# A decoder step with expert retrieval: 192 gathered tokens instead of 128, 352 columns through the whole tables instead of 416, three row buffers instead of two

## The chip, the cores and the metric

The kernel runs on one core of a Trainium2 chip. Its time is the device time of one execution in microseconds (us). The core has TensorE (PE, with its weight loads shown apart as PEld), VectorE (DVE), ScalarE (ACT), GpSimd (POOL), SyncE (SP, which issues most DMAs) and 16 DMA engines. Each engine works through its own list of instructions in order.

## The reference

One decoder layer for 544 tokens of width 2048: 512 tokens of a prompt and 8 x 4 sample tokens. First come a norm, an input projection, a gated MLP over positions, an RWKV-7 mixer and an output projection. Then comes the part that the change touches: `peer_ffn`, a product-key retrieval of experts, and after it a residual sum and a norm.

```python
q = (xt @ w_q).reshape(n_tok, 8, 2, 128)
s = einsum('nhcd,ckd->nhck', q, sub_keys)           # 2 x 128 key scores per head
top_s, top_i = top_k(s, 16)                         # then the best 16 of 16 x 16 sums
...
ue = u_tab[e_b]                                     # 16384 x 2048 table, 128 rows a token
act = gelu(einsum('nhkd,nd->nhk', ue, x_b))
coef = gates * act
out = einsum('nhk,nhkd->nd', coef, v_tab[e_b])
```

So each token needs 128 rows of `u_tab` (a dot product with its own normed activation) and the same 128 rows of `v_tab` (a weighted sum). Each table holds 134 MB in float32.

## The kernel before

The kernel has two ways to do this and splits the tokens between them.

**Whole tables (tokens 0 to 415, `T1` = 416 columns).** TensorE multiplies all 16384 rows with the 416 tokens, and a matrix of gates that is zero almost everywhere picks the few that count. The first table is read in 128 blocks of 128 experts (`activations`, L750): 48 matmuls of 416 columns a block, into one PSUM bank; DVE multiplies by the norm's factor (L755), ACT takes the gelu. The second table is read in 32 groups of 4 blocks and 8 pairs of column tiles (`products`, L1048): 24 matmuls of 416 columns a call, after which DVE adds two banks to `yT` (L1065). Between them `coefficients` (L1031) multiplies activations by gates on POOL (L1041) and splits them into two float32r parts (ACT L1044, POOL L1045). All weights go through `split` (L647): a DMA of 512 KB on SP's queue into one of three `wr` buffers, a cast on ACT (`wh`) and a subtraction on DVE (`wl`, L655). Each product is then three matmuls (hi x hi, hi x lo, lo x hi), which is why there are 48 and 24.

**Gathered rows (tokens 416 to 543, `TG` = 128).** They go in waves of 32 tokens (`gather_steps`, L776): 4 groups of slots x 32 tokens fill the 128 partitions, so that a wave has 32 steps on `u_tab` and 32 on `v_tab`. One step fetches 128 rows of 8 KB (1 MB) with an indirect DMA that POOL issues (`fetch`, L793), and works on the row block fetched the step before: `dot` (L805) or `add` (L813), one DVE instruction over 128 x 2048. There are two row buffers (`row`, bufs=2). Step 8 of the next wave runs `finish` (L838), which sums the four groups of slots with four small matmuls, adds the residual and norms; it takes two of the row buffers for its own operands, loaded through SP's queue.

**What sets the order.** `gathers(n, after)` (L866) counts fractions of steps and hands out a step when a whole number is reached; the fetch and the row's DVE instruction get a dependency on `after`, the DVE instruction that has just emptied a bank. A step is handed out for each early block (`EW` = 1); in the last stage the steps that are left are spread over `products` calls (weight 4) and `activations` calls (weight 6) with a factor `PACE` = 1.06, so that they end when 1/1.06 of the stage is done. A planner then orders each engine's list by priority.

**The stages behind the mixers.** 1159 to 1263 us: second half of the output projection, norm 2, the gathered tokens' rows written to memory (`hn` the residual, `xg` the normed row). 1263 to 1487: queries and scores; the last 128 tokens have theirs with tokens on partitions. 1487 to 1918: top-k of the other tiles on DVE; TensorE works on early blocks (`early`, L764; 52 blocks of the first table before their gates exist, written to `Cd`). 1918 to 2204: the gate matrix, in 13 groups of 32 tokens (L1002 to L1016: 16 comparisons on DVE, a multiplication on POOL, matmuls), each group followed by one early block. 2204 to 2254: the early blocks that are left. 2254 to the end: `coefficients` and `products`.

Of the kernel before, what the change touches and what calls it, by code (L numbers as in the profile page):

```python
# [15 lines left out]
D = 2048  # L16
# [12 lines left out]
# columns of the constants' array  # L29
# [38 lines left out]
def front(tc, I, O, SC, dbg=None):  # L68
    """norm1, input projection, both mixers; leaves y^T in SC['yT']."""
# [54 lines left out]
        # the sample's tokens; the states before them are normalised already  # L124
# [23 lines left out]
    def weights(src, k0, n):  # L148
        """part of a weight tile, split into two float32r parts that add up to it"""
# [9 lines left out]
    # ---------------- projection of one column tile: 2 halves in PSUM  # L159
# [16 lines left out]
    # ---------------- A: v half, LayerNorm, mixing over positions  # L176
# [88 lines left out]
    # halved biases for sigmoid(z) = 0.5 tanh(z/2) + 0.5  # L265
# [14 lines left out]
    def seg(p, s, q, lora, st):  # L280
# [17 lines left out]
        # decay: log w = -E05 sigmoid(.)  # L298
# [18 lines left out]
        # normalised kk  # L317
# [10 lines left out]
        # k (1 + (a - 1) k_a)  # L328
# [24 lines left out]
        # V with tokens on partitions: even head's rows 64.., odd head's rows ..64  # L353
# [19 lines left out]
        # B, K with tokens on partitions  # L373
# [7 lines left out]
        # inner products  # L381
        # E[:, 0] holds N^T on the rows of its head, E[:, 1] the keys' part on the other head's
# [37 lines left out]

        # L = ((I - N)^-1)^T by merging diagonal blocks, Ti = L^T
# [5 lines left out]
        # blocks of at most 32 rows: their transposes stay within the blocks  # L427
# [14 lines left out]
        # the states  # L442
# [63 lines left out]
        # group norm, bonus, gate  # L506
# [46 lines left out]
    # ---------------- h = x + y_A w_out[:W_A] + .., the first half of the sum  # L553
# [34 lines left out]
TG = 128  # L588
T1 = TC - TG
HT = TC // 2  # L590
NW = TG // 32
GT = 32
GB = 4
EARLY = 52
# [8 lines left out]
def back(tc, I, O, SC):  # L603
    """output projection, norm2, PEER, final norm."""
# [33 lines left out]
    # top-k results by token tile: gates and the two key numbers  # L638
# [8 lines left out]
    def split(wp, src, ahead, E=V):  # L647
        """1024 columns of weights, split into two float32r parts that add up to them"""
# [34 lines left out]
    ms = rsp.tile([TG, 1], F32, name="ms")  # L683
    with ExitStack() as s1:
# [5 lines left out]
        xh = x2.tile([128, KT, T1], F32R, name="xh2")  # L690
        xl = x2.tile([128, KT, T1], F32R, name="xl2")
        xt = pool(xts, "xt", side="right")
        th = xt.tile([128, KT, TG], F32R, name="th")
        tl = xt.tile([128, KT, TG], F32R, name="tl")
# [7 lines left out]
        hn = hp.tile([TG, D], F32, name="hn")  # L702
        ss = hp.tile([128, TC], F32, name="ss")
        for m in range(KT):
# [13 lines left out]
            if m % 4 == 0:  # L718
                pxt = px.tile([128, 512], F32, name="pxt")
# [5 lines left out]
            for hi, lo, c in ((xh, xl, slice(0, T1)), (th, tl, slice(T1, TC))):  # L725
# [7 lines left out]
        # the gathered tokens' rows, normalised  # L733
        G.dma_start(SC["hn"], hn)
# [474 lines left out]
```

## Time and profile before

| | us |
|---|---|
| time, median of 3 runs (lowest, highest) | 4234.88 (4228.41, 4239.51) |
| the profiled execution: span from first to last instruction | 4256.0 |
| PE busy | 3973.8 (93%) |
| PEld busy | 3741.6 (88%) |
| DVE busy | 2894.4 (68%) |
| POOL busy | 1508.2 (35%) |
| ACT busy | 1329.7 (31%) |
| mean granted TensorE clock | 0.969 |
| moved by DMA | 760.39 MB |

The profile's page gives one execution, and of that one only the span; no time outside the span is shown for it. Busy time of PE counts a matmul from its start to a modelled end, and matmuls overlap, so that a busy PE is not a PE at its peak: the number of matmuls in a stretch (the x behind its busy time) says more. The DMA share is the mean busy share of the core's 16 DMA engines.

### The profile page before, as it was taken

Reading aid. Unit: us, or ns where it says so; the run is one execution under the profiler, and the core shown is the slowest. Engines: PE = TensorE matmul, PEld = TensorE weight load, DVE = VectorE, ACT = ScalarE, POOL = GpSimd, SP = SyncE. Lnnn points to the kernel's source line nnn. Section 1 sums busy time; section 2 is a strip of 40 time slices with the busy share of each in tenths; the row PEclk is TensorE's granted clock in tenths of the full one; section 3 lists DMA queues with packets and bytes.
Section 4 is the critical chain, followed back from the end, with each engine's and each line's share of the span. In section 5 each row is a group of like instructions: output and inputs, shape, how many; then the busy total and the mean of one; then the engine's idle time right before and its main releaser. Section 6 shows DMA issues by size and latency. Waiting matters only on the chain. (4 is left out here: it accounts for less than half of the span.)

```text
span 4256.0 us, 65074 instructions
## 1 busy us (share of the span) xinstructions
PE 3973.8 (93%) x25618; PEld 3741.6 (88%) x25618; DVE 2894.4 (68%) x4763; ACT 1329.7 (31%) x2137; POOL 1508.2 (35%) x1222
## 2 busy tenths in 40 slices
PE   8999999999999988788889899999999999999997
PEld 8888888887999987787789899899898998999997
DVE  4566666666455599979984766666666666766754
ACT  4244444444232222223332222222222222322233
POOL 1212222222160056576653334343343333433323
PEclk9999999997999999999999999999999999999998
DMA  4311111112553245465566767777677776776752
GB/s 150 105 56 58 59 57 57 58 56 77 189 163 97 77 140 196 168 229 215 204 233 221 262 237 256 244 263 258 229 253 258 248 249 240 263 254 246 257 177 90
DMA packets 240241, 760.39 MB, mean 179 GB/s; under 512 B 23240, under 2 KB 88520, under 8 KB 204224
## 3 DMA queue, kind: packets, MB, share of 16 engines
q1 hardware_dynamic: 191136, 427.57, 30.9%
q0 software_dynamic: 48800, 328.67, 20.5%
q8 instruction: 202, 3.31, 0.3%
q14 instruction: 103, 0.84, 0.1%
HBM read 692.53 MB, written 63.61 MB: 178 GB/s over the span
## 5 line engine op out<-in xcount | busy, mean ns | idle before, releaser
L654 ACT CAST wh<-wr 128x1024 fp32r<-128x1024 f32 x560 | 581.5, 1048 | 1248.0 <-PE o L1057 545.7
L655 DVE TENSOR_TENSOR wl<-wr,wh 128x1024 fp32r<-128x1024 f32 x488 | 618.2, 1268 | 319.2 <-ACT wh L654 318.4
L668 PE MATMUL g<-xh,wh 128*128 128x416 f32 x2048 | 733.1, 358 | 67.1 <-DVE ac L755 67.0
L1057 PE MATMUL o<-ch,wh 128*128 128x416 f32 x2048 | 740.1, 361 | 48.3 <-ACT ch L1044 41.8
L1057 PE MATMUL o<-cl,wh 128*128 128x416 f32 x2048 | 740.1, 361 | 35.9 <-POOL cl L1045 35.9
L668 PE MATMUL g<-xh,wl 128*128 128x416 f32 x2048 | 733.9, 358 | 3.5 <-POOL wl L655 3.5
L1057 PE MATMUL o<-ch,wl 128*128 128x416 f32 x2048 | 733.5, 358 | 0.0
L668 PE MATMUL g<-xl,wh 128*128 128x416 f32 x2048 | 726.4, 355 | 0.0
L668 PEld LDWEIGHTS g<-xh,wh 128*128 128x128 f32 x2048 | 392.6, 192 | 78.1 <-issue 75.2
L1057 PEld LDWEIGHTS o<-ch,wh 128*128 128x128 f32 x2048 | 398.3, 194 | 64.3 <-ACT ch L1044 48.9
L1057 PEld LDWEIGHTS o<-cl,wh 128*128 128x128 f32 x2048 | 395.8, 193 | 47.5 <-POOL cl L1045 44.8
L805 DVE SCALAR_TENSOR_TENSOR row<-row,xrow 128x2048 f32<-128x2048 f32 x128 | 309.2, 2416 | 167.8 <-DMA row<-in_u_tab,idx 166.8
L1057 PEld LDWEIGHTS o<-ch,wl 128*128 128x128 f32 x2048 | 396.3, 194 | 7.3
L793 POOL DMA_INDIRECT row<-in_v_tab,idx x128 | 231.4, 1808 | 480.6 <-DVE y L1065 295.4
L668 PEld LDWEIGHTS g<-xh,wl 128*128 128x128 f32 x2048 | 391.5, 191 | 8.6 <-POOL wl L655 5.2
L668 PEld LDWEIGHTS g<-xl,wh 128*128 128x128 f32 x2048 | 392.8, 192 | 6.4
L813 DVE SCALAR_TENSOR_TENSOR acc<-row,dots,acc 128x2048 f32<-128x2048 f32 x124 | 296.3, 2389 | 147.4 <-DMA row<-in_v_tab,idx 145.5
L171 PE MATMUL g<-xh,wh 128*128 128x276 f32 x1248 | 379.3, 304 | 10.0 <-ACT xh L113 10.0
L793 POOL DMA_INDIRECT row<-in_u_tab,idx x128 | 221.8, 1733 | 445.0 <-DVE y L1065 288.1
L171 PE MATMUL g<-xl,wh 128*128 128x276 f32 x1248 | 375.9, 301 | 0.2 <-DVE xl L114 0.2
L171 PE MATMUL g<-xh,wl 128*128 128x276 f32 x1248 | 374.6, 300 | 0.0
L1065 DVE TENSOR_TENSOR y<-o,y 128x416 f32<-128x416 f32 x496 | 273.7, 584 | 111.0 <-PE o L1057 110.5
(687 smaller groups left out, 6781.7 us busy)
## 6 DMA issues: line engine op xcount, KB each, us to landing
wr<-in_uT SPq DMA_DIRECT2D x256, 512.0 KB, 5.0
wr<-in_vT SPq DMA_DIRECT2D x256, 512.0 KB, 4.4
wr<-in_w_in SPq DMA_DIRECT2D x172, 256.0 KB, 3.0
Gd<-st POOLq DMA_DIRECT2D x13, 2048.0 KB, 7.1
gl<-Gd SPq DMA_DIRECT2D x32, 832.0 KB, 5.4
wr<-in_w_q SPq DMA_DIRECT2D x32, 512.0 KB, 3.6
Cd<-ac POOLq DMA_DIRECT2D x52, 208.0 KB, 4.6
ac<-Cd SPq DMA_DIRECT2D x52, 208.0 KB, 5.7
```

The costliest lines, as they stand in the source:

```text
L171: T.matmul(ps[:M, :HC], a, b[:, k, c], start=n == 0, stop=n == 3 * KT - 1)
L654: A.copy(hi, raw)
L655: E.tensor_sub(lo, raw, hi)
L668: T.matmul(ps[:, :N], a, b[:, k, c], start=n == 0, stop=n == 3 * KT - 1)
L793: d = G.indirect_dma_start(out=u, out_offset=None, in_=tab, in_offset=bass.IndirectOffsetOnAxis(ap=idx[w][:, r:r + 1], axis=0))
L805: i = V.scalar_tensor_tensor(u, u, 1.0, xrow, op0=OP.mult, op1=OP.mult, accum_out=dots[w][:, r:r + 1])
L813: i = V.scalar_tensor_tensor(acc, u, dots[w][:, r:r + 1], acc, op0=OP.mult, op1=OP.add)
L1057: T.matmul(ps[j][:, :T1], a, x_, start=i + n == 0, stop=i == GB - 1 and n == 2)
L1065: last = V.tensor_add(yT[:, m], ps[j][:, :T1], prev)
```

## The change

`TG` goes to 192, so 352 columns (`TD`) go through the whole tables. The queries keep their old split (416 and 128 columns, now `TQ` and `TT`). Tokens 352 to 415 are gathered as well, so there are six waves; the one with tokens 352 to 383 comes last, because its top-k result comes last. The gate matrix has 11 groups. There are three row buffers, a row is worked on two steps after its fetch, and each wave ends with two steps that only work off the queue (66 steps a wave, 396 in all; before 64 a wave and 9 at the end, 265). `finish` comes at step 12 and, for the last wave, right at its end. The gathered rows are written to memory by quarters inside the output projection's loop, without the norm's factor, which goes to memory as `ms` and is applied to the dot products in the gelu's `scale`. Some scratch tiles of the top-k have one buffer instead of two. Comments were taken out all over the file.

```diff
-TG = 128
-T1 = TC - TG
+TG = 192
+TD = TC - TG
+TT = 128
+TQ = TC - TT
+ROWS = 3
+WAVES = sorted(range(TD, TC, 32), key=lambda c: (c < 384, c))
+GROUPS = [(TQ, TT)] + [(c, min(TQ - c, 128)) for c in range(TD, TQ, 128)]
+STEPS = (64 + ROWS - 1) * NW
...
-            T.transpose(pxt[:TG, m % 4 * 128:m % 4 * 128 + 128], h_[:, T1:], C("ident"))
+            for g, (c, n) in enumerate(GROUPS):
+                T.transpose(pxt[g][:n, m % 4 * 128:m % 4 * 128 + 128], h_[:, c:c + n], C("ident"))
             if m % 4 == 3:
-                A.copy(hn[:, m // 4 * 512:m // 4 * 512 + 512], pxt[:TG])
+                for g, (c, n) in enumerate(GROUPS):
+                    hn = hp.tile([128, 512], F32, name="hn", bufs=2)
+                    A.copy(hn[:n], pxt[g][:n])
+                    G.dma_start(SC["hn"][c - TD:c - TD + n, qs], hn[:n])
+                    xg = hp.tile([128, 512], F32, name="xg0", bufs=2)
+                    A.activation(xg[:n], hn[:n], AF.Square, accum_out=sg[g][:n, m // 4:m // 4 + 1])
+                    V.tensor_mul(xg[:n], hn[:n], gb[:n])
+                    G.dma_start(SC["xg"][c - TD:c - TD + n, qs], xg[:n])
...
-    ps = gemm(wp, pg, I["uT"][b], xh, xl, [slice(0, T1)], ahead, E=E)[0]
+    ps = gemm(wp, pg, I["uT"][b], xh, xl, [slice(0, TD)], ahead, E=E)[0]
...
+        msw = gp[0].tile([128, 1], F32, name="msw", bufs=2)
         for j in range(4):
-            S.dma_start(xrow[j * 32:j * 32 + 32],
-                        SC["xg"][w * 32:w * 32 + 32])
+            S.dma_start(xrow[j * 32:j * 32 + 32], SC["xg"][c - TD:c - TD + 32])
+            S.dma_start(msw[j * 32:j * 32 + 32], SC["ms"][c - TD:c - TD + 32])
...
-            u = gp[0].tile([128, D], F32, name="row", bufs=2)
+            u = gp[0].tile([128, D], F32, name="row", bufs=ROWS)
...
+        def work_on(u, r, after):
+            if r < 32:
+                dot(u, r, after)
+            else:
+                add(u, r - 32, after)
+            if r == 31:
+                A.activation(dots[w], dots[w], AF.Gelu, scale=msw)
+                V.tensor_mul(dots[w], dots[w], gts[w])
...
+        for r in range(64):
+            after = yield
+            if r == 12 and w:
+                finish(w - 1)
+            queue.append((fetch(I["u_tab" if r < 32 else "v_tab"], r % 32, after), r))
+            if len(queue) == ROWS:
+                work_on(*queue.pop(0), after)
+        while queue:
+            after = yield
+            work_on(*queue.pop(0), after)
...
-    NG = T1 // GT
+    NG = TD // GT
...
-                            T.matmul(ps[j][:, :T1], a, x_, start=i + n == 0,
+                            T.matmul(ps[j][:, :TD], a, x_, start=i + n == 0,
...
-        left = 64 * NW + 8 - work[0]
+        left = STEPS - work[0]
```

## Rows read from the trace of the kernel before

**Rows 1.** The page's 40 slices of the span (106.4 us each): busy share in tenths.
```profile
PE   8999999999999988788889899999999999999997
...
DVE  4566666666455599979984766666666666766754
...
DMA  4311111112553245465566767777677776776752
```

**Rows 2.** Busy time by stage. Columns: stretch in us, its length, then busy us and number of instructions of PE, PEld, DVE, ACT, POOL, then granted TensorE clock, DMA share, GB/s.
```profile
1159.00:1263.00 104.00, 101.67 (x790) 99.18 (x788) 54.03 (x78) 36.63 (x63) 65.23 (x45) 1.00 0.52 160
1500.00:1800.00 300.00, 240.90 (x1156) 229.59 (x1154) 299.71 (x744) 70.45 (x84) 172.75 (x89) 0.92 0.51 170
1850.00:1918.00 68.00, 68.00 (x364) 67.33 (x363) 37.00 (x35) 19.77 (x24) 57.07 (x29) 1.00 0.80 269
1918.00:2204.00 286.00, 241.82 (x1489) 224.15 (x1488) 280.72 (x265) 96.08 (x150) 191.64 (x144) 0.96 0.55 206
2204.00:2254.00 50.00, 50.00 (x267) 49.55 (x265) 21.89 (x19) 16.23 (x21) 17.08 (x15) 1.00 0.79 272
2254.00:4256.00 2002.00, 1895.08 (x9685) 1843.23 (x9683) 1303.81 (x1329) 551.60 (x654) 724.03 (x479) 0.97 0.68 237
```

**Rows 3.** The same view of two stretches in which TensorE never waits at full clock: matmuls of 272 columns (L668 and its like in the output projection), and of 416 columns (L1057, L668).
```profile
1120.00:1140.00 20.00, 20.00 (x161) 20.00 (x160) 9.08 (x18) 4.93 (x8) 1.62 (x3) 1.00 0.71 230
3675.00:3705.00 30.00, 30.00 (x160) 29.67 (x159) 19.12 (x22) 8.48 (x11) 11.06 (x8) 1.00 0.77 270
```

**Rows 4.** Groups of matmuls in the last stage (2254 to 4256 us), the first of three of each line: line, engine, operation, names, shape, count, busy us, mean ns, idle time before and what ended it.
```profile
L1057 PE MATMUL o<-ch,wh 128*128 128x416 f32 x2048 | 740.1, 361 | 48.3 <-ACT ch L1044 41.8 <-DVE y L1065 6.4
...
L668 PE MATMUL g<-xh,wl 128*128 128x416 f32 x1169 | 412.6, 353 | 0.0
```

**Rows 5.** Groups of DVE instructions in the last stage, the same columns.
```profile
L655 DVE TENSOR_TENSOR wl<-wr,wh 128x1024 fp32r<-128x1024 f32 x400 | 502.3, 1257 | 241.6 <-ACT wh L654 240.9
L1065 DVE TENSOR_TENSOR y<-o,y 128x416 f32<-128x416 f32 x496 | 273.7, 584 | 111.0 <-PE o L1057 110.5
L813 DVE SCALAR_TENSOR_TENSOR acc<-row,dots,acc 128x2048 f32<-128x2048 f32 x109 | 259.9, 2385 | 141.3 <-DMA row<-in_v_tab,idx 139.9
L805 DVE SCALAR_TENSOR_TENSOR row<-row,xrow 128x2048 f32<-128x2048 f32 x96 | 221.2, 2305 | 147.9 <-DMA row<-in_u_tab,idx 147.0
L755 DVE TENSOR_TENSOR ac<-g,rs 128x416 f32<-128x416 f32 x74 | 43.1, 582 | 30.2 <-PE g L668 30.2
...
L848 DVE TENSOR_TENSOR row<-row,o 32x512 f32<-32x512 f32 x16 | 9.9, 669 | 0.0
...
L853 DVE SCALAR_TENSOR_TENSOR row<-row,ms 32x2048 f32<-32x2048 f32 x4 | 9.4, 2339 | 0.1
```

**Rows 6.** One DVE line of the output projection: shortest, median and longest ns, first and last start, shape (an addition from PSUM of 272 columns).
```profile
L710 DVE TENSOR_TENSOR h<-g,xr x32: 423/427/442, 1162.8 to 1263.2; 128x272 f32<-128x272 f32 x32
```

**Rows 7.** Waits in the last stage, 2254 to 4100 us: who waited for whom, us in total, times, longest.
```profile
DVE row L805 <- DMA row<-in_u_tab,idx: 147.0, 66, 6.3
DVE acc L813 <- DMA row<-in_v_tab,idx: 139.9, 65, 4.8
```
```profile
PE o L1057 <- ACT ch L1044: 41.4, 18, 5.6
PE o L1057 <- POOL cl L1045: 35.2, 27, 5.1
```

**Rows 8.** One late row, in order of time: start us, length, engine, line, and in brackets the idle time before and what ended it.
```profile
2680.78 2.29 DVE L805 SCALAR_TENSOR_TENSOR row<-row,xrow 128x2048 f32<-128x2048 f32 x1 [3.04 <-DMA row<-in_u_tab,idx]
...
2684.75 0.55 ACT L756 ACTIVATE ac<-ac 128x416 f32<-128x416 f32 x1 [11.80 <-DVE ac L755]
...
2687.06 0.71 PE L1057 MATMUL o<-ch,wh 128*128 128x416 f32 x1 [4.81 <-ACT ch L1044]
```

**Rows 9.** The fetches (L793) between 2300 and 4100 us: POOL's instruction (shortest, median, longest ns) and the time from issue to landing.
```profile
L793 POOL DMA_INDIRECT row<-in_v_tab,idx x109: 932/1677/2967, 2302.8 to 4082.0; - x109
...
DMA to landing us min/median/max: 5.2/7.6/11.6
```

**Rows 10.** DMA in the last stage: the whole traffic, and issues (count, KB each, median us to landing).
```profile
DMA packets 149948, 474.77 MB, mean 237 GB/s; under 512 B 11760, under 2 KB 71882, under 8 KB 122698
...
gl<-Gd SPq DMA_DIRECT2D x29, 832.0 KB, 5.4
...
row<-in_v_tab,idx POOLq DMA_INDIRECT x111, 7.6
row<-in_u_tab,idx POOLq DMA_INDIRECT x96, 7.6
```

**Rows 11.** The two stretches of 20 and 25 us with the highest DMA share in the last stages (columns as in rows 2), and the GB/s of 40 slices of 0.6 us from 2600 to 2625 us.
```profile
2220.00:2240.00 20.00, 20.00 (x107) 19.82 (x106) 11.65 (x9) 5.63 (x7) 5.85 (x5) 1.00 0.95 334
3625.00:3650.00 25.00, 22.98 (x122) 22.44 (x121) 18.43 (x16) 8.95 (x11) 13.94 (x9) 1.00 0.93 329
```
```profile
GB/s 433 419 367 406 269 354 419 426 341 328 433 229 170 393 288 197 321 406 374 387 380 347 98 170 170 295 446 439 341 419 328 26 52 210 275 459 459 406 402 376
```

**Rows 12.** DVE's comparisons for the gate matrix, 1918 to 2204 us (columns as in rows 4).
```profile
L1010 DVE TENSOR_TENSOR Rt<-CT,eT 128x512 f32<-128x512 f32 x104 | 142.5, 1370 | 0.0
L1010 DVE TENSOR_TENSOR Lt<-CT,eT 128x512 f32<-128x512 f32 x104 | 80.7, 776 | 0.0
```

More of the change, by code (lines that the diff above doesn't have):

```diff
@@ L682, in back @@
     rs2 = rsp.tile([128, TC], F32, name="rs2")
-    ms = rsp.tile([TG, 1], F32, name="ms")
+    ms = rsp.tile([TT, 1], F32, name="ms")
     with ExitStack() as s1:
@@ L701, in back @@
             V.tensor_sub(yl[:, k], r, yh[:, k])
-        hn = hp.tile([TG, D], F32, name="hn")
         ss = hp.tile([128, TC], F32, name="ss")
+        sg = [hp.tile([128, 4], F32, name=f"sg{g}") for g in range(len(GROUPS))]
         for m in range(KT):
@@ L814, in add @@
             late(i, after)
-        u = None
-        for r in range(32):
+        for r in range(64):
             after = yield
-            if r == 8 and w:
+            if r == 12 and w:
                 finish(w - 1)
-            n = fetch(I["u_tab"], r, after)
-            if r:
-                dot(u, r - 1, after)
-            u = n
-        after = yield
-        n = fetch(I["v_tab"], 0, after)
-        dot(u, 31, after)
-        u = n
-        A.activation(dots[w], dots[w], AF.Gelu)
-        V.tensor_mul(dots[w], dots[w], gts[w])
-        for r in range(1, 32):
+            queue.append((fetch(I["u_tab" if r < 32 else "v_tab"], r % 32, after), r))
+            if len(queue) == ROWS:
+                work_on(*queue.pop(0), after)
+        while queue:
             after = yield
-            n = fetch(I["v_tab"], r, after)
-            add(u, r - 1, after)
-            u = n
-        add(u, 31, after)
+            work_on(*queue.pop(0), after)
     def finish(w):
         acc = rows[1]
-        hr = gp[0].tile([128, D], F32, name="row", bufs=2)[:32]
-        S.dma_start(hr, SC["hn"][w * 32:w * 32 + 32])
-        gb = gp[0].tile([128, D], F32, name="row", bufs=2)[:32]
+        o = WAVES[w] - TD
+        hr = gp[0].tile([128, D], F32, name="row", bufs=ROWS)[:32]
+        S.dma_start(hr, SC["hn"][o:o + 32])
+        gb = gp[0].tile([128, D], F32, name="row", bufs=ROWS)[:32]
         S.dma_start(gb, bass.AP(tensor=I["fg"].tensor, offset=I["fg"].offset, ap=[[0, 32], [1, D]]))
@@ L858, in all_steps @@
             yield from gather_steps(w)
-        for r in range(8):
-            yield
         finish(NW - 1)
@@ L868, in gathers @@
         work[0] += n if steps else 0
-        while nstep[0] < min(64 * NW + 9, int(work[0])):
+        while nstep[0] < min(STEPS, int(work[0])):
             nstep[0] += 1
@@ L995, in back @@
         gs_ = pool(s1, "gs", 2)
-        eT = gs_.tile([128, 3, TP], F32, name="eT", bufs=1)
-        for t in range(4):
+        eT = gs_.tile([128, 3, NE * 128], F32, name="eT", bufs=1)
+        for t in range(NE):
             p_ = pt.tile([128, 512], F32, name="p_")
@@ L1021, in back @@
     yp = pool(es, "y")
-    yT = yp.tile([128, KT, T1], F32, name="y")
+    yT = yp.tile([128, KT, TD], F32, name="y")
     with ExitStack() as s1:
@@ L1036, in coefficients @@
             if b in firsts:
-                ac = cp.tile([128, T1], F32, name="ac")
+                ac = cp.tile([128, TD], F32, name="ac")
                 S.dma_start(ac, SC["C"][firsts.index(b)])
@@ L1062, in products @@
                 if g == 0:
-                    prev = vp.tile([128, T1], F32, name="hr")
-                    S.dma_start(prev, SC["hT"][m][:, :T1])
-                last = V.tensor_add(yT[:, m], ps[j][:, :T1], prev)
+                    prev = vp.tile([128, TD], F32, name="hr")
+                    S.dma_start(prev, SC["hT"][m][:, :TD])
+                last = V.tensor_add(yT[:, m], ps[j][:, :TD], prev)
                 if g == NGR - 1:
@@ L1080, in back @@
             if b == 128:
-                ss.append(vp.tile([128, T1], F32, name="hr"))
+                ss.append(vp.tile([128, TD], F32, name="hr"))
             if b < 128:
@@ L1090, in back @@
         pss = po[0].tile([128, 512], F32, name="o")
-        T.matmul(pss[:, :T1], C("ones"), ss[0], start=True, stop=True)
-        rs = cp.tile([128, T1], F32, name="ac")
-        A.activation(rs, pss[:, :T1], AF.Sqrt, bias=eps, scale=1.0 / D)
+        T.matmul(pss[:, :TD], C("ones"), ss[0], start=True, stop=True)
+        rs = cp.tile([128, TD], F32, name="ac")
+        A.activation(rs, pss[:, :TD], AF.Sqrt, bias=eps, scale=1.0 / D)
         V.reciprocal(rs, rs)
```

85 lines of the change are left out of this document (43 added, 42 removed).

## The prediction

> **What bounds the kernel now.** I read the 40 slices first [rows 1]: PE is at 9 tenths nearly everywhere, DVE reaches 9 only in slices 14 to 20, and DMA lies at 6 or 7 tenths over the second half. The table by stage [rows 2] says which engine ends each stage. From 1500 to 1800 us DVE is busy 299.7 of 300 us and PE gets through only 1156 matmuls: DVE bounds the top-k. From 1850 to 1918 and from 2204 to 2254 PE is busy throughout at full clock. From 1918 to 2204 DVE bounds again (280.7 of 286). The last stage, 2254 to 4256, is 47% of the span: PE does 9685 matmuls there, DVE is 65% busy and DMA 68%.
>
> The busy time of a matmul overlaps the next one's, so I take its price from stretches without a wait [rows 3]: 30 us / 160 = 187.5 ns for 416 columns, 20 us / 161 = 124.2 ns for 272. The last stage holds 3 x 2048 + 3 x 1169 = 9651 matmuls of 416 columns [rows 4], or 1810 us. With some 25 us at the end for the last norm, 1835 of its 2002 us are TensorE at full speed and about 167 are lost. Where they go is in the waits [rows 7]: DVE stands 147 + 140 us before row blocks that have not landed, and PE waits 41 + 35 us for coefficients. One late row shows the link [rows 8]: DVE waits 3.0 us for a row, takes 2.3 us for it, only then empties the bank behind it, ACT's gelu had been idle for 11.8 us, and PE starts its product 4.8 us late. So PE is the bound, with a loss that comes from two row buffers.
>
> **The change, part by part.** I name the stages A (to 1487 us), B (to 1918), C (to 2254) and D (to 4256).
>
> *Stage A.* Everything to 1159 us is untouched. In the output projection there are 16 transposes more, small copies and squares on ACT, eight multiplications on DVE, and 16 or so more DMA issues on POOL; PE is busy 101.7 of 104 us there while ACT has 67 us free, DVE 50 and POOL 39 [rows 2]. They are hidden, 0 us; were that cover gone, the transposes alone would cost at most 16 x 0.124 = 2 us, as much as 272 columns each [rows 3], and I keep 5. Less work follows behind the projection, which lies beside the first queries: 0.
>
> *Matmuls of 352 columns.* 352 lies between the two measured widths, so 124.2 + 80 x 63.3/144 = 159.4 ns, 28.1 ns less than now [rows 3]; both ends being measured, I allow 3 ns.
>
> *Stage B.* Where DVE bounds, a shorter matmul gives nothing; 27 evictions get shorter by 0.07 us (from 584 ns at 416 columns and 427 at 272 [rows 5, 6], 514 at 352): 2 us. From 1850 to 1918 PE bounds: 364 x 28.1 ns = 10 us. B: -12 us (-2 to -30, if the faster matmuls also shorten the DVE-bound part).
>
> *Stage C.* The 208 comparisons take 223 us [rows 12], 17.2 us for each of 13 groups, and the stage 286 / 13 = 22 us a group with the early block's own DVE work. Two groups go: -44 us. Their two early blocks are then done after the gates, where PE bounds: 2 x 48 x 159.4 ns = +15 us, and the 267 matmuls there get shorter, -7.5 us [rows 2]. C: -36 us (-25 to -45).
>
> *Stage D* has three walls, and the change moves all of them. The gathers are spread so that they end after 1/1.06 = 94.3% of the stage's matmuls; the last 5.7%, and the last 25 us, have no gathers in them.
>
> PE: 9651 x 159.4 ns = 1538 us instead of 1810.
>
> DVE: `wl` stays at 502 us. 512 + 75 evictions at 514 ns are 302. Of 6 x 64 = 384 row blocks, 47 are worked on before the stage (256 - 208 now, and one less because of the longer queue), so 337 are left instead of 208: 160 dot products at 2.39 us (with the read of the sum) and 177 additions at 2.385 are 804. Six closings at (9.9 + 9.4)/4 and a bit, 5 us, are 30 [rows 5]. Sum 1638 and 13 for the last norm. The same sum for now gives 1354 where the stretch shows 1304 [rows 2], since neighbours overlap; scaled, 1590. About 60 of these fall behind the gathers: 1530 us until the gathers end, 88 of matmuls, 25 of closing. DVE's wall is 1643.
>
> DMA: 474.8 MB are moved now, 207 fetches of 1.05 MB among them [rows 10]. There will be 335 fetches, +134 MB, and the gates, stored activations and residuals shrink by 15% (gates 24.7 MB), -6: 603 MB, some 585 of them before the gathers end. The stage moves 237 GB/s at a share of 0.68, so 349 at a full share; the fullest stretches, 334 at 0.95 and 329 at 0.93, say 352 and 354 [rows 2, 11]. I take 350: 585 MB need 1671 us, and with 88 and 25 the wall is 1784.
>
> So DMA becomes the highest wall, DVE is near it, and PE falls to the lowest. How near a share of 1 can it come? Nothing here shows 100 us of it. Three row buffers keep two fetches under way while one is worked on, and three `wr` buffers keep weights asked for, so the engines should seldom lack work: I take the fullest measured share, 0.95, over the gathers: 1759 + 113 = 1872 us for D, -130. Ends: 1784 (share 1) and 1960 (share 0.905, half way down to the 0.863 at which, as worked out below, nothing is gained).
>
> The third buffer itself: a buffer is taken from issue to the end of its row's work, 7.6 us to landing [rows 9] and 2.3 us of DVE [rows 5]. Two buffers allow a step each 5.0 us at the median; the new pace wants 335 fetches in some 1760 us, 5.25 us each, with no room for a late one. Three allow 3.3 us at the median, and 4.6 at the longest landing seen (11.6). So the 287 us of DVE's row waits should shrink although the rows come faster; what is late next is the transfer itself. The new waits: each wave's two steps without a fetch (12 steps of 396, inside the steps counted), and `finish`, whose two loads stand on SP's queue until a row buffer is free, weights behind them; there are six of these instead of four, with one buffer more. I put that at 0 (+10 a piece if PE runs dry: +20).
>
> Sum for the profiled execution: 4256 - 12 - 36 - 130 = 4078. Its span lies 21 us above the median of the runs and nothing is shown around it, so the time is 4078 - 21 = 4057, rounded to **4060 us**, 4.1% less.
>
> **The rivals.**
>
> *DVE is the wall, DMA is not (chance 0.2, 3985 us).* A packet's time holds waits for other packets, so the share may overstate how full the engines are. For it: slices of 0.6 us reach 433 to 459 GB/s [rows 11]. Against: no stretch of 20 us got above 334. Then D is DVE's 1643 and as much loss as now, about 160: 1803, -199, hence 4256 - 12 - 36 - 199 - 21 = 3988. The Trainium skill, "Perfetto Trace Analysis", section "Roofline", speaks for this rival: it has a single active core exceed the per-core 358 GB/s and calls about 120% the practical ceiling. By that, 430 GB/s, the transfers would want 1361 us and be no wall; the trace agrees for slices of 0.6 us and for nothing longer.
>
> *DMA is the wall and cannot be kept full (0.15, 4150 us).* Rows and weights land at odd times, PE idles in between and its clock falls, as in 1500 to 1800 us where PE at 80% had a granted clock of 0.92 [rows 2]. With a share of 0.90, D is 585/315 = 1857 + 113 = 1970; -32 leaves 4155.
>
> *Rows and weights get in each other's way: slower (0.13, 4340 us).* Place: stage D, the 16 DMA engines. Price: at a mean share s, D is 1671/s + 113. It decides from D = 2002 + 48 = 2050, that is s = 0.863: below it the kernel is slower than now. For it: the 106-us slices of now show 6 and 7 tenths, never 8 in the last half [rows 1], though weights are always asked for ahead. Against: that is now what was asked for, as the gathers are paced. At 0.82, D is 2151, +149, and the time 4256 - 48 + 149 - 21 = 4336.
>
> *No change (0.07):* s about 0.863.
>
> The forecast itself has the other 0.45.
>
> **How the numbers follow.** A measurement of this kernel can tell about 0.3%, 13 us, from no change. Faster: 0.45 + 0.2 + 0.15 = 0.80; same 0.07; slower 0.13. The forecast alone ranges from 3970 (share 1) to 4145 (0.905). Downward the DVE rival with half its loss, 3910, is left out in part; upward the range takes in the underfilled DMA and stops short of no change: 3950 to 4200. Outside it lie some 0.05 below and 0.15 above.
>
> **What would show it.** Right: matmuls of 352 columns 159 ns apart where PE does not wait; C shorter by about 36 us, the first 1487 us unchanged within 5; in D a DMA share above 0.9 and 330 GB/s or more while gathers run, DVE busy around 85%, PE's matmuls with gaps; DVE's wait for a row less than 0.86 us a row on average, which is what 287 us over 335 rows would be. Wrong: a share that stays at 0.8 with a longer stage D (the slower rival), D at 1800 with DVE above 88% and landings still near 7.6 us (the DVE rival), 352 columns costing more than 163 ns, or a landing above 13 us at the median with weights late behind it.

## The result and the profile after

The kernel after takes 4131.0 us (median of 4 runs, 4120.8 to 4142.8), the one before 4237.2 beside it: a ratio of 0.974, 95% interval 0.970 to 0.978. That is faster, and within the range, but 106 us less instead of the 177 forecast. The profiled execution has a span of 4119.0 us against 4256.0. On the page the second half has changed:

```profile
PE   8999999999999987778898798889889888889997
...
DVE  4566666667555589999976888888888887888995
...
DMA  4211111112553236656576899889989888998993
```

Against [rows 1], DVE and DMA went from 6 and 7 tenths to 8 and 9, and PE fell from 9 to 8: no engine is full any more. The busy time by stage, with the columns of [rows 2]; the stages are cut at the same instructions as before (output projection, queries, top-k, gates, products):

```profile
1142.60:1254.70 112.10, 104.89 (x808) 101.68 (x806) 68.96 (x92) 46.85 (x89) 78.36 (x64) 0.99 0.60 192
1254.70:1473.10 218.40, 215.13 (x1306) 206.67 (x1305) 114.49 (x395) 51.07 (x98) 8.83 (x6) 0.99 0.25 77
1473.30:1881.00 407.70, 323.12 (x1788) 312.30 (x1786) 403.81 (x919) 107.99 (x137) 279.45 (x138) 0.91 0.58 192
1881.00:2167.60 286.60, 247.27 (x1588) 236.42 (x1589) 260.66 (x249) 97.53 (x146) 179.82 (x137) 0.94 0.63 233
2167.80:4119.00 1951.20, 1690.22 (x9700) 1633.10 (x9698) 1610.93 (x1536) 553.84 (x668) 857.22 (x612) 0.93 0.86 311
3800.00:4000.00 200.00, 188.52 (x1138) 186.40 (x1138) 186.83 (x167) 60.22 (x71) 102.04 (x65) 0.96 0.95 355
```

In the profile before, these stages begin at 1159.5, 1263.7, 1487.9, 1921.9 and 2254.4 us (their first matmul; for the gates DVE's first comparison). The 137 us between the spans divide so:

| | before | after | difference | forecast |
|---|---|---|---|---|
| up to the output projection | 1159.5 | 1142.6 | -17 | 0 |
| output projection | 104.2 | 112.1 | +8 | 0 |
| queries | 224.2 | 218.6 | -6 | 0 |
| B, top-k | 434.0 | 407.7 | -26 | -12 |
| C, gates | 332.5 | 286.8 | -46 | -36 |
| D, products | 2001.6 | 1951.2 | -50 | -130 |

The 17 us in front are none of the change. The same stretch of work in the mixers ran at a granted clock of 0.64, most of it at half clock, in the profiled execution of before, with 486 matmuls where the other gets 646 through:

```profile
1000.00:1060.00 60.00, 59.69 (x486) 47.59 (x485) 32.00 (x101) 16.44 (x40) 8.86 (x17) 0.64 0.15 44
```
```profile
1000.00:1060.00 60.00, 59.01 (x646) 48.04 (x646) 41.41 (x127) 20.13 (x49) 10.78 (x21) 1.00 0.25 73
```

(first before, then after). Nine of the twelve kernels tried below, which are the kernel after up to here, show a granted clock of 0.57 to 0.65 in the same 60 us; `half_both`, `uw8` and `tg160_pace` show 0.99 or 1.00, as the kernel after does.

In D the waits show what took the place of the old ones: who waited for whom, us in total, times, longest.

```profile
PE o L1071 <- DVE y L1079: 127.2, 51, 8.3
...
DVE wl L662 <- ACT wh L661: 99.1, 88, 5.2
DVE row L819 <- DMA row<-in_u_tab,idx: 92.8, 49, 6.9
...
DVE acc L838 <- DMA row<-in_v_tab,idx: 54.0, 37, 4.8
...
PE o L1071 <- POOL cl L1059: 48.5, 27, 4.9
```

The waits for rows halved, 287 to 147 us, although 335 rows come instead of 207 [rows 7]. In their place PE waits 127 us for DVE to empty a bank, which cost it 6.4 us before [rows 4]. The order of one such stop (columns as in [rows 8]):

```profile
3008.78 2.29 DVE L819 SCALAR_TENSOR_TENSOR row<-row,xrow 128x2048 f32<-128x2048 f32 x1 [6.88 <-DMA row<-in_u_tab,idx]
...
3011.66 0.40 PE L1071 MATMUL o<-ch,wh 128*128 128x352 f32 x1 [1.25 <-DVE y L1079]
...
3012.56 2.28 DVE L819 SCALAR_TENSOR_TENSOR row<-row,xrow 128x2048 f32<-128x2048 f32 x1
...
3015.35 0.43 PE L1071 MATMUL o<-ch,wh 128*128 128x352 f32 x1 [2.01 <-DVE y L1079]
...
3016.34 2.28 DVE L819 SCALAR_TENSOR_TENSOR row<-row,xrow 128x2048 f32<-128x2048 f32 x1
...
3019.22 0.40 PE L1071 MATMUL o<-ch,wh 128*128 128x352 f32 x1 [1.21 <-DVE y L1079]
```

DVE stands 6.9 us before a row that has not landed. Then it works without a pause, a row, an eviction and a weight split in turn, and PE stops at three products running. With DVE busy for 83% of D instead of 65%, there is little slack to catch up with.

Waits are not all that D loses. At 157.2 ns (worked out below) its 9700 matmuls are 1525 us of the 1951; PE is idle for 261 us, and its busy time of 1690 is 165 above the 1525, at a granted clock of 0.93 (before: 1816 us at 187.5 ns, busy 1895, 0.97). No run tells what D would be with these stops and the full clock.

### The profile page after: what moved, and what is told of

It reads as the page before. It is cut to its first block, busy times and chain, and to the rows that moved or that the text cites. A ratio compares the mean times of both kernels' runs of the same rounds, so it can differ in the third digit from the quotient of the medians.

```text
span 4119.0 us, 65426 instructions
## 1 busy us (share of the span) xinstructions
PE 3673.2 (89%) x25519; PEld 3450.7 (84%) x25519; DVE 3178.2 (77%) x4962; ACT 1324.8 (32%) x2151; POOL 1634.2 (40%) x1350
## 4 chain that ended last, share of the span: by engine, by line
PE 44%; DVE 19%; issue 15%; DMA 10%; POOL 10%; ACT 1%; SPq 0%; DVEq 0%; POOLq 0%; ACTq 0%
PE g L171 10%; PE o L1071 9%; PE g L675 7%; DMA row<-in_v_tab,idx 4%; PE q L970 4%; POOL row L807 3%; DMA row<-in_u_tab,idx 3%; DVE row L819 3%; POOL ac L1055 2%; PE i L419 2%; POOL cl L1059 2%; DVE wl L662 2%; PE g L573 2%; PE i L171 1%; DVE cd L923 1%
## 5 line engine op out<-in xcount | busy, mean ns | idle before, releaser
L1071 PE MATMUL o<-ch,wh 128*128 128x352 f32 x2048 | 692.4, 345 | 178.6 <-DVE y L1079 127.2
L675 PE MATMUL g<-xh,wh 128*128 128x352 f32 x2048 | 683.3, 334 | 83.5 <-DVE ac L768 77.7
L1071 PE MATMUL o<-cl,wh 128*128 128x352 f32 x2048 | 699.2, 342 | 48.5 <-POOL cl L1059 48.5
L1071 PE MATMUL o<-ch,wl 128*128 128x352 f32 x2048 | 691.9, 339 | 0.7 <-DVE wl L662 0.7
L675 PE MATMUL g<-xh,wl 128*128 128x352 f32 x2048 | 677.4, 331 | 12.2 <-POOL wl L662 7.4
L675 PE MATMUL g<-xl,wh 128*128 128x352 f32 x2048 | 674.5, 329 | 0.0
L819 DVE SCALAR_TENSOR_TENSOR row<-row,xrow 128x2048 f32<-128x2048 f32 x192 | 464.2, 2418 | 93.8 <-DMA row<-in_u_tab,idx 92.8
L838 DVE SCALAR_TENSOR_TENSOR acc<-row,dots,acc 128x2048 f32<-128x2048 f32 x186 | 456.7, 2455 | 55.2 <-DMA row<-in_v_tab,idx 54.0
L807 POOL DMA_INDIRECT row<-in_u_tab,idx x192 | 308.0, 1604 | 474.2 <-DVE y L1079 250.6
L662 POOL TENSOR_TENSOR wl<-wr,wh 128x1024 fp32r<-128x1024 f32 x72 | 196.3, 2736 | 224.8 <-ACT wh L661 223.9
```

The source lines that it names most:

```text
L662: E.tensor_sub(lo, raw, hi)
L675: T.matmul(ps[:, :N], a, b[:, k, c], start=n == 0, stop=n == 3 * KT - 1)
L807: d = G.indirect_dma_start(out=u, out_offset=None, in_=tab, in_offset=bass.IndirectOffsetOnAxis(ap=idx[w][:, r:r + 1], axis=0))
L819: i = V.scalar_tensor_tensor(u, u, 1.0, xrow, op0=OP.mult, op1=OP.mult, accum_out=dots[w][:, r:r + 1])
L838: i = V.scalar_tensor_tensor(acc, u, dots[w][:, r:r + 1], acc, op0=OP.mult, op1=OP.add)
L1071: T.matmul(ps[j][:, :TD], a, x_, start=i + n == 0, stop=i == GB - 1 and n == 2)
```

## The experiments

Twelve kernels were run, each beside runs of the kernel before. Their planners order the work anew, since they count costs, so an edit can change the order elsewhere, too. All in one table; the columns from "D" on are read from the stretch from the first product to the end of the profiled execution. Ratios are those to the kernel before, whose median was 4250 to 4257 us in these runs.

| run | ratio (95%) | D, us | PE busy | DVE busy | DMA share, GB/s |
|---|---|---|---|---|---|
| before | 1 | 2001.6 | 1895 | 1303 | 0.68, 237 |
| after | 0.974 (0.970-0.978) | 1951.2 | 1690 | 1611 | 0.86, 311 |
| rows2 | 1.034 (1.030-1.038) | 2216.0 | 1752 | 1609 | 0.78, 274 |
| tg128r | 0.977 (0.974-0.981) | 1905.3 | 1858 | 1311 | 0.71, 249 |
| tg160r | 0.967 (0.962-0.972) | 1888.7 | 1758 | 1455 | 0.79, 286 |
| rows4 | 0.966 (0.962-0.970) | 1925.8 | 1686 | 1623 | 0.86, 315 |
| half_fetch | 0.949 (0.945-0.953) | 1865.0 | 1658 | 1609 | 0.71, 231 |
| half_dve | 0.953 (0.949-0.957) | 1911.3 | 1660 | 1232 | 0.86, 318 |
| half_both | 0.910 (0.906-0.914) | 1709.8 | 1612 | 1205 | 0.76, 252 |
| pace102 | 0.968 (0.963-0.973) | 1934.0 | 1666 | 1612 | 0.87, 314 |
| uw8 | 0.974 (0.970-0.977) | 1955.0 | 1690 | 1625 | 0.86, 310 |
| rows4_uw8 | 0.964 (0.959-0.968) | 1914.7 | 1680 | 1636 | 0.87, 317 |
| rows4_uw8_pool | 0.971 (0.968-0.975) | 1938.5 | 1670 | 1607 | 0.86, 313 |
| tg160_pace | 0.959 (0.956-0.961) | 1846.7 | 1743 | 1457 | 0.80, 293 |

### The two parts of the change apart

The change does two things, more gathered tokens and a third buffer. `rows2` takes the buffer back, and with it a row is worked on one step after its fetch again:

```diff
-ROWS = 3
+ROWS = 2
```

> Two row buffers instead of three, all else as in the kernel after. Theory (a row that lands late is what stops VectorE): with one row less under way the waits of VectorE for rows rise from 146 us to 250 or more, and the time by 20 to 90 us. Rival (the third buffer is worth nothing, as the forecast had it): within 12 us of the kernel after.

It is 3.4% slower than the kernel before. Its waits in D:

```profile
POOL row L807 <- DVE row L819: 381.2, 101, 9.7
POOL row L807 <- DVE acc L838: 302.2, 80, 6.9
...
PE o L1071 <- DVE y L1079: 266.6, 81, 12.2
...
DVE row L819 <- DMA row<-in_u_tab,idx: 212.4, 110, 7.9
...
DVE acc L838 <- DMA row<-in_v_tab,idx: 202.3, 114, 6.8
```

The next fetch waits 683 us for a buffer (168 with three), so rows are late by 415 us (147), and PE waits 267 us behind them (127). D is 265 us longer; the whole time is 256 us above the kernel after by the ratios, where the expectation had 20 to 90.

`tg128r` is the other half: 128 tokens and 416 columns as before, with a third buffer. There was no room for one, so its 8 KB are those of the chosen scores and indices (`bv`, `e1`, `e2`), whose last reading for all waves moves to the start of the second wave; from there on, behind the first product, three buffers take turns.

```diff
-TG = 192
+TG = 128
-ROWS = 3
+ROWS = 2
-    bv = res.tile([128, ntile, 8, 16], F32, name="bv")
...
+    rx = res.tile([128, D], F32, name="rx")
+    bv, e1, e2 = (rx[:, i * 640:i * 640 + 640].rearrange("p (t h k) -> p t h k", t=ntile, h=8)
+                  for i in range(3))
...
+        for v in range(1, NW) if w == 1 else ():
+            choose(v)
...
-            u = gp[0].tile([128, D], F32, name="row", bufs=ROWS)
+            nf[0] += w >= 1
+            u = rx if nf[0] % 3 == 1 else gp[0].tile([128, D], F32, name="row", bufs=ROWS)
...
+        deep = ROWS + (w >= 1)
...
-            if len(queue) == ROWS:
+            if len(queue) == deep:
```

(`choose` holds the lines of `gather_steps` that fill `idx` and `gts`.)

> The third buffer alone: 128 tokens gather as in the kernel before, 416 go through the tables, and from the second wave on, behind the first product, three row buffers take turns (the third one's 8 KB are those of the chosen scores and indices). Theory (the third buffer is what gains, and 192 tokens with two buffers cost 3.4%): the waits for rows, 147 + 140 us in the kernel before, fall under 100 and the time falls by 60 to 150 us from the kernel before. Rival (with a third less rows there is room between them already, share 0.87): within 30 us of the kernel before.

0.977, 102 us less than before. D's window and the waits for rows that are left:

```profile
2247.10:4152.40 1905.30, 1857.54 (x9684) 1818.53 (x9682) 1311.13 (x1328) 553.30 (x654) 830.92 (x479) 0.99 0.71 249
```
```profile
DVE acc L847 <- DMA row<-in_v_tab,idx: 33.8, 19, 4.5
...
DVE row L828 <- DMA row<-in_u_tab,idx: 13.5, 10, 2.7
...
DVE acc L847 <- DMA rx<-in_v_tab,idx: 8.4, 5, 3.4
```

The row waits fall from 287 us to 67 (two shorter lines for `rx` make up the rest), and TensorE is busy for 97.5% of D at a clock of 0.99. So the third buffer alone brings nearly all that the whole change brings. (`tg128r` keeps the kernel after's smaller edits, the rows written by quarters and the later `finish`; no run takes those apart from the buffer.) The 64 tokens more, on top of it, bring 0.3% (0.977 to 0.974), and these intervals overlap; without the third buffer, 192 tokens cost 3.4% against the kernel before. The faster matmuls are there in full, but what they free is not used in D: D is 46 us longer with the 64 tokens (1951.2 against 1905.3). What they save lies before it: D begins at 2167.8 us instead of 2247.1, of which 17 us are the half clock and some 62 are theirs, 45 in the gates and 17 in front of them.

### What holds D up at 192 tokens

`half_fetch` lets a row bring only half its bytes while DVE's work stays whole; `half_dve` fetches whole rows and works on half of each; `half_both` does both. What is left out belongs to all gathered tokens, not to the sample tokens alone.

```diff
-            d = G.indirect_dma_start(out=u, out_offset=None, in_=tab,
+            d = G.indirect_dma_start(out=u[:, 1024:], out_offset=None, in_=tab.rearrange("n (a d) -> (n a) d", a=2),
...
-            i = V.scalar_tensor_tensor(u, u, 1.0, xrow, op0=OP.mult, op1=OP.mult,
+            i = V.scalar_tensor_tensor(two(u), u[:, None, 1024:].to_broadcast([128, 2, 1024]), 1.0, two(xrow), op0=OP.mult, op1=OP.mult,
```

(`half_fetch`; `two` is a view as 2 x 1024, and the additions are edited likewise)

> Each gathered row brings 4 KB of its 8 KB, and VectorE still works on 2048 columns (it reads the 1024 that came twice; the sampled tokens' feed-forward output is therefore not the reference's). The 335 gathers that fall behind the first product then move 176 MB less of the 607 MB there. Theory (from the first product to the end, the transfers and VectorE bind together, the transfers first): that stage falls from 1951 us to 1700-1830, the waits of VectorE for rows (146 us) and of TensorE for evictions (127 us) mostly go. Rival (VectorE alone binds, its 1611 us busy and the time lost by its order): the stage stays within 1900-1951. The planner's order changes too, since it counts a gather by its bytes.

```diff
-            i = V.scalar_tensor_tensor(u, u, 1.0, xrow, op0=OP.mult, op1=OP.mult,
+            i = V.scalar_tensor_tensor(u[:, :1024], u[:, :1024], 1.0, xrow[:, :1024], op0=OP.mult, op1=OP.mult,
```

(`half_dve`, and the same for `acc` from the second row of a wave on)

> The fetch is whole, and VectorE's product and sum over a row take 1024 of the 2048 columns (the other columns of the sampled tokens' feed-forward are left out). VectorE's busy time behind the first product falls from 1611 us to some 1220. Theory (the transfers bind first, share 0.89 with whole rows): that stage falls by no more than 50 us from 1951, the share of the transfers rises by as much as the time falls. Rival (VectorE binds): it falls by 150 us or more, to 1800 or less, and the transfers go over 340 GB/s. In between: the two bind in turn. The selection of experts, where VectorE is busy 99%, gets shorter in either case by half of the 81 + 34 us of row work there.

> Rows of 4 KB and VectorE's work on 1024 columns together (the other half of the sampled tokens' feed-forward is left out). If transfers and VectorE are all that hold TensorE up, the stage from the first product to the end falls from 1951 us to 1650-1750 (some 9790 matmuls of 159.4 ns are 1561 us, and the head, the end and the half clock come on top). If it stays at 1830 or more, near the 1865 that half the bytes alone gave, TensorE's own stops (clock, the coefficients from GpSimd, the order) are the rest.

D alone is to be read, since `half_dve` and `half_both` gain in the top-k too. Half the bytes take 86 us off D, short of the 121 to 251 expected and more than the 0 to 51 of the rival. Half of DVE's row work takes 40, as the theory of the transfers had it, but the transfers' share did not rise with it (0.86 in both). Both together take 242, inside what was expected, where the sum of the two would be 126. The three windows:

```profile
2191.50:4056.50 1865.00, 1657.59 (x9699) 1604.27 (x9698) 1608.79 (x1536) 549.98 (x666) 889.80 (x609) 0.95 0.71 231
```
```profile
2155.00:4066.30 1911.30, 1659.89 (x9700) 1612.57 (x9698) 1232.00 (x1537) 553.85 (x669) 761.16 (x613) 0.93 0.86 318
```
```profile
2139.80:3849.60 1709.80, 1611.85 (x9700) 1574.25 (x9698) 1204.57 (x1536) 550.25 (x666) 824.93 (x609) 0.97 0.76 252
```

With one of the two relieved, the other holds D. In `half_fetch` DVE is busy for 86% and PE waits 119 us for evictions, nearly as in the kernel after. In `half_dve` that wait is 11 us, but DVE waits 378 us for rows, and PE 204 us for coefficients:

```profile
ACT wh L661 <- DMA wr<-in_uT: 313.6, 90, 7.5
...
DVE row L819 <- DMA row<-in_u_tab,idx: 197.6, 115, 6.2
...
DVE acc L838 <- DMA row<-in_v_tab,idx: 175.0, 107, 6.3
...
PE o L1071 <- POOL cl L1059: 113.5, 36, 7.7
...
PE o L1071 <- ACT ch L1058: 90.5, 33, 7.8
...
PE o L1071 <- DVE y L1079: 10.6, 10, 3.2
```

Those coefficients start from weights, and ACT waits 314 us there for weights of the first table to land, against 87 in the kernel after; that the one wait makes the other is read from these lines and not tried. Only with both relieved is TensorE the bound again, busy 94% of D. So at 192 tokens D has two bounds close together, the transfers first and DVE right behind them.

### A fourth buffer, and where the gathers lie

`rows4` is the kernel after with a fourth buffer from the second wave on, taken from the same place as in `tg128r`.

```diff
+            nf[0] += w >= 1
+            u = rx if nf[0] % 4 == 1 else gp[0].tile([128, D], F32, name="row", bufs=ROWS)
```

> A fourth row buffer from the second wave on, which begins behind the first product (its 8 KB are those of the chosen scores and indices, read out for all waves by then). Theory (how long a row takes to land under load, times how few rows are under way, is what stops VectorE, and VectorE then TensorE): the step from two buffers to three took 280 us off; a fourth takes the waits of VectorE for rows from 146 us to under 70 and those of TensorE for evictions from 127 to under 80, and the time falls by 20 to 80 us from the kernel after. Rival (the transfers are at their limit already, at share 0.89): within 20 us of it, and the waits move to the weights.

0.966, and the interval just clears that of the kernel after. The 25 us in D are within what was expected, but the path is not. (The 280 us that the expectation gives for the step from two buffers to three are 256 by the ratios.) The waits for rows go, as forecast; the wait for evictions stays:

```profile
PE o L1081 <- DVE y L1089: 123.7, 52, 6.0
...
DVE rx L828 <- DMA rx<-in_u_tab,idx: 22.5, 5, 7.3
...
DVE acc L847 <- DMA row<-in_v_tab,idx: 18.0, 12, 2.9
...
DVE row L828 <- DMA row<-in_u_tab,idx: 9.1, 7, 3.1
```

So late rows are not what most of those 127 us hang on; DVE's load is, as `half_dve` showed, where that wait was 11 us. And ACT waits 191 us for weights of the second table instead of 155, which fits rows that are asked for earlier and take their transfers' time. From 2400 to 3600 us the share is 0.90 with three buffers and with four, at 323 and 328 GB/s (lines at the end).

`pace102` and `uw8` change the density of the gathers, the one over the stage (`PACE` 1.06 to 1.02), the other between products and activations (`UW, VW` 6, 4 to 8, 4).

> PACE 1.02 instead of 1.06: the gathers are spread over 4% more of the products. Theory (where gathers and products run together the transfers bind): that stretch moves faster per product by up to 4% of 335 gathers x 1.05 MB over 326 GB/s, some 40 us, which the end then lacks; time 10 to 30 us less than the kernel after. Rival (no bound is the density, only the sum): within 10 us.

> Only UW 8 instead of 6: more of the gathers go to the blocks of activations, fewer to the products. From the rows of the kernel after: a product takes TensorE 24 x 159.4 ns = 3.83 us, and VectorE one split of 1.33, two evictions of 0.51 and 0.97 rows of 2.4, 4.7 us, while 1.55 MB are to come (404 GB/s); a block of activations takes TensorE 7.65 us, VectorE 6.7 us, and 2.6 MB come (336 GB/s). With UW 8 a product has 0.88 rows: 4.5 us and 1.45 MB (378 GB/s); a block 1.77 rows: 7.4 us and 2.9 MB. Theory (the stage from the first product to the end loses its time where products ask for more than VectorE and the transfers give, and doesn't get it back in the blocks): 256 products x up to 0.2 us, 15 to 60 us less than the kernel after. Rival (only the sums over the stage count): within 12 us.

`pace102` has 0.968 (D -17), `uw8` 0.974 (D +4). The first leans towards its theory, but its interval overlaps that of the kernel after: not settled. The second theory falls: this other split of the gathers between products and blocks of activations changes nothing clear of the noise. What evens it out was not tried.

`rows4_uw8` has four buffers, `PACE` 1.02 and `UW` 8. `rows4_uw8_pool` moves every fourth weight split of a product to GpSimd besides:

```diff
-            ws = split(wp, I["vT"][g, m2], 300)
+            ws = split(wp, I["vT"][g, m2], 300, G if m2 % 4 == 3 else V)
```

> Four row buffers from the second wave on, PACE 1.02 and UW 8 together. If the three gains add (four buffers 0.966 against 0.974, PACE 0.968, UW 8 as forecast for it) the ratio to the kernel before is 0.945 to 0.958; if they take off the same waits, 0.960 to 0.968.

> As the one with four buffers, PACE 1.02 and UW 8, and every fourth split of a product's weights is subtracted on GpSimd (64 x 2.4 us there, 64 x 1.33 us less on VectorE: 4.2 us a product instead of 4.5). Theory (VectorE's order behind a row is what stops TensorE, waits for evictions 124 us): 10 to 50 us less than without. Rival (GpSimd, 47% busy, delays coefficients and fetches by 2.4 us each time): the waits for coefficients rise from 57 us and the time is the same or up to 40 us more.

0.964: the gains don't add. With GpSimd's help 0.971, slower, as its rival had it; the intervals just touch, but every execution is longer than the longest without. The wait for evictions falls from 83.5 to 45.5 us, and the one for GpSimd's coefficients, 72.7 us without, takes its place:

```profile
PE o L1081 <- POOL cl L1069: 121.0, 34, 10.1
```

### Fewer tokens, with the third buffer

> 160 tokens gather, 384 go through the tables, three row buffers from the second wave on. Between the two: a matmul of 384 columns by the two measured ones some 173 ns, 9790 of them 1694 us; rows behind the first product some 275 against 335. If the transfers bind at 192 tokens, this is 10 to 60 us faster than the kernel after; if TensorE's columns count in full, it is 50 to 130 us slower.

> 160 tokens gather, 384 go through the tables, two row buffers, three from the second wave on, PACE 1.02. With 160 tokens and PACE 1.06 the stage from the first product to the end took 1888.7 us, TensorE busy 1757.6 of them against a bound of 9790 matmuls x 173 ns = 1694 us, and no engine and no transfer stood above 0.93 of it. Theory (what is left are late rows and the coefficients behind them, 81 and 81 us, and 4% fewer rows to a product takes part of them): the stage 1850-1880, the ratio to the kernel before 0.958 to 0.965, the fastest of all that compute the whole. Rival (TensorE's own columns and clock bind with 160 tokens): 0.965 to 0.972, the same as with PACE 1.06.

Both are `tg128r` with `TG` 160 (384 columns), the second with `PACE` 1.02. 160 tokens give 0.967, by the medians' ratios 28 us less than the kernel after, as the theory of the transfers had it; the intervals overlap. The second gives 0.959 (0.956 to 0.961) and is the fastest of all that compute the whole, 1.6% below the kernel after and 176 us below the one before.

```profile
2210.00:4056.70 1846.70, 1743.01 (x9691) 1710.06 (x9689) 1456.54 (x1432) 550.49 (x658) 852.83 (x544) 0.97 0.80 293
```

TensorE is busy for 94% of D, the transfers' share is 0.80, and PE waits 14 us for evictions. Here the spread does tell: 42 us of D (3 more than the theory's most), with intervals that do not meet. Its reason is only in part the one expected: the waits for coefficients fall from 81 to 64 us (GpSimd's part from 67 to 47, ACT's rises from 14 to 17), those for rows (`rx` included, which the 81 us of the expectation left out) hardly, from 113 to 103. The granted clock of D rose from 0.96 to 0.97. At the same `PACE` of 1.02, 192 tokens have 0.968 and 160 have 0.959, and these intervals do not meet either.

## Why the prediction was right, and where it was off

**What bounds the kernel before.** Right, and now shown: the loss of TensorE came from two row buffers. `tg128r` removes most of it and leaves TensorE 97.5% busy. (DVE reaches 9 tenths in slices 15 to 20 of [rows 1], not 14 to 20; nothing hangs on it.)

**The matmul of 352 columns.** Forecast 159.4 ns. From 3900 to 3925 us PE is busy throughout at full clock with 159 of them: 25 / 159 = 157.2 ns. Right.

**A.** Forecast 0 and at most 5; the projection is 8 us longer, the queries 6 shorter, which cancels. One thing was not priced: PE waits 4.7 us for GpSimd's sum of squares before norm 2 (`n` L750 behind `ss` L724).

**B and C.** -12 and -36 forecast, -26 and -46 measured. Both signs and the reason (two groups of comparisons fewer) hold; B lies in its range, C just outside. Some 7 us in front of the gates come without the 64 tokens: `tg128r`, with the same half clock as before, begins them at 1915.0 us instead of 1921.9.

**D.** This is the step that failed in size: -130 forecast, -50 measured, 79 us too much. Its terms: 606.9 MB are moved (603 forecast). The last fetch starts at 4016.8 us, so the part without gathers takes 102 us (113 forecast). In between, the stretch with gathers takes 1849 us at a share of 0.89 and 321 GB/s, where the forecast had 1759 at 0.95 and 332. So the mis-sized term is the mean rate of the transfers, through their share: 62 of the 90 us are 321 GB/s instead of 332, and 28 are bytes, 594 MB instead of 585. The share was taken from stretches of 20 and 25 us [rows 11] and asked of 1800 us. (At a share of 0.89 the 321 make 361 at a full share, where the forecast had 350: that part erred the other way.)

```profile
2167.80:4016.80 1849.00, 1612.78 (x9260) 1560.73 (x9259) 1555.86 (x1471) 513.74 (x609) 826.70 (x584) 0.94 0.89 321
```

Such stretches are there after, too, and fuller (3000 to 3025 us has a share of 1.00); the mean is not. How the 79 divide between transfers and DVE is not settled: with DVE's row work halved, D is 1911, 40 us less and 39 above the forecast, but half the bytes alone take 86, and the two effects do not add. The prediction put DVE's wall at 1643, PE's at a full clock, and treated the highest wall as the time. DVE's busy time was nearly right (1590 forecast, 1611 measured), but with two walls 9% apart the higher one did not set the time alone: a late row stops DVE, and DVE then has little in hand to catch up. PE's busy time came to 1690, where its wall has 1538 (here with a granted clock of 0.93).

**The third buffer.** "0 (+20)" was right only for the `finish` loads that it spoke of. As a part of the change it was never priced: it is 265 us of D at 192 tokens (`rows2`) and 96 at 128 (`tg128r`). So the forecast had the sign of D right in part by luck: it gave D's gain to the faster matmuls, and the runs give it to the buffer, 96 us, of which the 64 tokens take 46 back. The formula of 5.0 us a step with two buffers was too kind: `rows2` gets its 335 rows only every 6.2 us (2092 us from the first fetch in D to the last). Landing (7.8 us there) and DVE's work (2.35) fill 10.2 of a buffer's 12.5 us; what fills the rest, a landed row's wait for its turn on DVE or the next fetch's for its own, was not taken apart.

**The rivals.** DVE alone as the wall (3985 us): refuted, half its row work gives 40 us. The transfers not kept full, 4150 us at a share of 0.90: nearest to what was measured, with 1970 for D against 1951, and its picture fits, PE idle in between at a clock of 0.93. Rows and weights obstructing each other until it is slower: not with three buffers; with two the kernel is slower, by 146 us, but from waits for buffers at a share of 0.78. 25 us of D reach 378 GB/s in the kernel after and 414 with a fourth buffer, so the 350 taken as a full rate was too low for short stretches; from 2400 to 3600 us no run with whole rows got above 328, and from 2750 to 3950 none above 333. The Trainium skill, "Perfetto Trace Analysis", section "Roofline", calls about 120% of 358 GB/s the practical ceiling of a single active core, an estimate of 430. The traces here come near it for 25 us (414) and for no stretch of 1200 us.

**The tests named.** 159 ns: met. C 36 us shorter: 46. The first 1487 us unchanged within 5: 15 shorter, for the half clock in the profile before. Row waits under 0.86 us a row: 147 / 335 = 0.44, met. DVE about 85% while gathers run: 1556 / 1849 = 84%, met. Share above 0.9 and at least 330 GB/s: missed, 0.89 and 321.

**Between profile and median.** The span's 137 us are 31 more than the medians' 106. 17 of them are the half clock in the profiled execution of before; the profiled execution of after is, besides, the fastest of its four.

## What to carry to other kernels

When a change does two things, price each alone, with the other left undone: here the tokens cost 3.4% without the buffer, the buffer gives 2.3% without the tokens, and both give 2.6%, so the two do not add; only both together were forecast. Where a change makes the bounds of a stage nearly equal, take off the highest one some per cent for the others (here 1951 against forecast walls of 1784, 1643 and 1538), and try a split that leaves one engine clearly the bound: here 160 tokens (TensorE busy 94% of D, 0.959), not 192 (0.968 at the same `PACE`). A share of transfers seen over 20 us is not one to plan 1800 us with.

## What the runs showed of the hardware

- Over 1200 us of mixed rows and weights the transfers came to 323 to 328 GB/s at shares of 0.89 and 0.90, in the kernel after, with a fourth buffer, and with DVE at half its row work (three lines, in this order).

```profile
2400.00:3600.00 1200.00, 1037.81 (x5913) 1004.73 (x5913) 1012.45 (x967) 328.71 (x390) 521.35 (x386) 0.93 0.90 323
```
```profile
2400.00:3600.00 1200.00, 1043.97 (x5984) 1011.07 (x5985) 1036.92 (x982) 329.25 (x393) 570.13 (x393) 0.94 0.90 328
```
```profile
2400.00:3600.00 1200.00, 1040.24 (x6059) 1015.67 (x6058) 776.51 (x977) 330.56 (x392) 481.77 (x390) 0.92 0.89 328
```

- 25 us alone go higher, and a share of about 1 is no fixed rate: 378 GB/s at 0.98 and 354 at 1.03 in the kernel after, 414 at 1.02 with a fourth buffer (third line).

```profile
3900.00:3925.00 25.00, 25.00 (x159) 25.00 (x158) 23.25 (x17) 8.30 (x11) 9.59 (x9) 1.00 0.98 378
2468.00:2493.00 25.00, 21.17 (x121) 20.59 (x120) 21.00 (x19) 8.23 (x12) 17.71 (x13) 0.93 1.03 354
```
```profile
3025.00:3050.00 25.00, 21.45 (x122) 20.84 (x122) 19.64 (x21) 7.08 (x8) 8.45 (x9) 0.93 1.02 414
```

- With 4 KB of a row instead of 8, the median time from issue to landing fell only from 9.0 and 9.1 us (the two tables, `half_dve`, whole rows) to 6.1 and 5.9 (`half_both`, the same DVE work): half the bytes, two thirds of the time. The share of the transfers fell with it, from 0.86 to 0.76.
- Some DVE row instructions take much longer than their usual 2.35 us. The one below, the longest of the additions, ran while GpSimd did a multiplication and two subtractions; in D the mean of the additions rose from 2385 ns [rows 5] to 2460, and that of the splits from 1257 to 1329. No run tried the cause. The Trainium skill, "SBUF — State Buffer", section "SBUF: two separate sides", has a DVE instruction with two SBUF inputs and a GpSimd instruction that reads SBUF take a port pair in turn, each for its whole length. The trace fits this here: DVE takes 2.13 us more beside 0.93 + 0.93 us of GpSimd, and the third GpSimd instruction, begun before DVE ended at 2609.28, takes 2.35 us instead of 0.93 and ends 0.79 us after DVE. No run here shows it apart.

```profile
2604.80 4.48 DVE L838 SCALAR_TENSOR_TENSOR acc<-row,dots,acc 128x2048 f32<-128x2048 f32 x1 [0.35 <-DMA row<-in_v_tab,idx]
...
2605.32 0.93 POOL L1059 TENSOR_TENSOR cl<-ac,ch 128x352 fp32r<-128x352 f32 x1
...
2606.20 0.93 POOL L1055 TENSOR_TENSOR ac<-ac,gl 128x352 f32<-128x352 f32 x1
...
2607.72 2.35 POOL L1059 TENSOR_TENSOR cl<-ac,ch 128x352 fp32r<-128x352 f32 x1 [0.60 <-ACT ch L1058]
```
